# Two blocks of turned rows that leave on other queues, in a one-core encoder layer

## The chip, the cores and the metric

The kernel runs on one core of one Trainium2 chip. A core has TensorE (PE in the profile, with its weight loads as PEld), VectorE (DVE), ScalarE (ACT), GpSimd (POOL) and SyncE (SP), and 16 DMA engines that all queues share. The metric is device time in microseconds of one launch; the time before is the median of three runs.

## The reference

One layer of an encoder over 2048 tokens of width 1024, all in float32. After windowed and neighbourhood attention with gates, the part that matters here is the end of the layer:

```
x  = x + merged @ w_out
h2 = rms_norm(x, norm_mlp)
x  = x + square(relu(h2 @ w_up)) @ w_down      # w_up: 1024 x 4096
return rms_norm(x, norm_final)
```

## The kernel before

**Products.** A float32 product is made of three TensorE products of float32r halves: each operand is split into a high part (a cast on ACT, L280) and a low part (a subtraction on DVE, L281), and L284 to L286 multiply high by high, high by low and low by high. On top of that the large products are cut 2 x 2 and made of seven products in place of eight, from sums and differences of the blocks. For `h2 @ w_up` the seven are numbered 1 to 7 and taken in the order 1, 5, 6, 2, 7, 4, 3 (`up_quad`, L1309).

**The stretch around the change.** The 2048 tokens are four blocks of 512. In the last part of the stage of `w_out`, for the two last blocks (2 and 3), the finished rows x are stored to x2d (L173, on ACT's queue), their squares are summed (L223, ACT; L226, DVE), the power -1/2 is taken (L228, POOL), and the rows are scaled (L235, ACT). They are then turned, features to partitions, since w_up's products contract over features. `turned_out` (L239) turns one block in four steps g of 256 columns: four DVE transposes of 32 x 32 squares (L247) fill one tile of 128 x 1024, and four transfers of 128 KB (L255) write its four groups of 32 partitions to the block's matrix in DRAM, `h2d`, in pieces of 512 bytes. Blocks 0 and 1 went that way earlier, from one tile `ht` and with SP's queue. Blocks 2 and 3 go through `turned_last` (L1468), with POOL's queue:

- block 2 is turned into the memory of two gate tiles, `m2` and `m3` (L1461), beside the last product of w_out;
- block 3 is turned into four tiles `hu` (L1532, L1538), after that stage's memory (`s_m`) has been given back.

So each block takes 16 transfers of 128 KB. POOL is in order: what stands behind such a transfer on POOL (the powers of block 3, L228) waits until it is issued.

**Memory that passes on.** The products with w_up take over that memory. Their right operands are pages `ubh1` to `ubh7`, one pair (high, low) for each product of the first group of tokens (blocks 0 and 1). `up_homes` makes them at three places: `bh1`, `bh5` first; `bh6`, `bh2` and the page `rb` after `s_m` is given back (L1530), partly where m2 and m3 were; `bh7`, `bh4`, `bh3` after hu and the rows are given back (L1541). A page can be written only when the transfers that read the memory before have ended.

**Weights.** w_up is taken in eight groups q of 512 columns for each of the two groups m of tokens. `up_weights(q)` (L1153) loads group q as two tiles `uraw` of 1 MB on SP's queue, one group ahead (L1557); `up_left` makes the seven left operands `uwhla`, `uwhlb` of them, with sums `uS`. The ring `uraw` has five tiles, which also hold pages while the right operands are made.

**Order.** A scheduler sets each engine's order when the program is built, by its own estimates of the times; `tc.issue_after(x)` holds an instruction back until x is issued in that order. All waits are on semaphores that the framework places; the transfers of SP's and ACT's queues take turns on eight of them, and a transfer is not issued before the last one on its semaphore has landed. TensorE's order around here is: the end of w_out's products (tiles `pgl`), then group q = 0 of w_up with products 1, 5, 2, 6, 7, 4 and 3.

Of the kernel before, what the change touches and what calls it, by code (L numbers as in the profile page):

```python
# [22 lines left out]
P = 128  # L23
KC = D // P
NB = 4
BT = 512
# [66 lines left out]
def encoder_layer(ctx, tc, x, norm_mix, w_in, b_gate, sink, rpb, w_pa, w_pb, w_out,  # L93
                  norm_mlp, w_up, w_down, norm_final, dist_a, mask_b, out):
    nc = tc.nc
    V, A, G, PE, SY = nc.vector, nc.scalar, nc.gpsimd, nc.tensor, nc.sync
# [114 lines left out]
    last_dma = [None]  # L211
# [27 lines left out]
    def turned_out(d, ht, tiles, g, gain=None, queue=None):  # L239

        hv = ht.rearrange("p (j t c) -> p t j c", j=8, t=4)
        for t in range(4):
            V.transpose(out=hv[:, t], in_=tiles[t][:, g * 256 : (g + 1) * 256].rearrange("p (j c) -> p j c", j=8))  # L247
        h3 = ht.rearrange("p (j x) -> p j x", j=8)
        if gain is not None:
            (step, n), _ = gain.ap  # L250
            gv = bass.AP(gain.tensor, gain.offset + 8 * g, [[step, n], [1, 8], [0, P]])
            V.tensor_tensor(out=h3, in0=h3, in1=gv, op=ALU.mult)
        dv = d.rearrange("(j i) (a x) -> a i j x", i=32, a=4)
        for a in range(4):
            (queue or SY).dma_start(dv[a][:, 8 * g : 8 * g + 8], h3[32 * a : 32 * a + 32])  # L255

    def turned_gain(t, norm):

# [33 lines left out]
    def ring(stack, tag, shape, dt, bufs, side="right"):  # L292

        pl = pool(f"r_{tag}", side=side, stack=stack)
        return lambda: T(pl, shape, dt, tag, bufs)
# [62 lines left out]
    def in_weights(c, w):  # L358

        return [row_half(c, w, p) for p in range(2)]  # L360
# [285 lines left out]
    ws = in_weights(*QUADS[2])  # L646
# [53 lines left out]
    for q in range(2, len(QUADS)):  # L700
        prep = iter(())
        if q in (2, 3):
            prep = wo_parts(q - 2, own_v)
        elif q in (7, 8):
            prep = wo_parts(q - 5, own_x)
        next(prep, None)
        if q == 5:
            s_v.close()
            in_v2.pop()
            xp = {**pools(s_z, "right", ("xin",), "x2"), "st": cp}  # L710
        if q == 7:
            bias_tables()
        lf = list(in_left(ws, 256, (1, 2) if q == 2 else (), ORDER if q == 2 else ORDER_3))
        if q + 1 < len(QUADS):
            ws = in_weights(*QUADS[q + 1])
        if q in (5, 6):

            b = q - 3
            xt = x_tiles(xp, b, 3)
            normalised(xp, xt, Junk(), by_scalar=True)  # L720
        ops2.extend(lf if q == 2 else ())
        for n, _ in enumerate(quad2 if q == 2 else in_seeded(*QUADS[q], iter(lf), right)):
            for _ in range(2 if q == 8 else 1):
                next(prep, None)
            if q in (5, 6) and n < 4:
                turned_out(h1d[b - 2], in_e().rearrange("p k x -> p (k x)"), xt, n)
        for _ in prep:
            pass
# [381 lines left out]
    h2d = [dp.tile([D, BT], F32, name=f"h2d{b}") for b in range(NB)]  # L1110
# [39 lines left out]
        n_whl[0] += 1  # L1150
        return (up_rings["whla"] if n_whl[0] % 3 == 1 else up_rings["whlb"])()

    def up_weights(q):  # L1153
        ws = []
        for p in range(2):
            w = up_rings["raw"]()
            SY.dma_start(w, w_up[0][p * BT : (p + 1) * BT, q * BT : (q + 1) * BT].rearrange("(k p) f -> p k f", p=P))
            ws.append(w)
        return ws

    def up_left(ws, behind=None):

        out = {}
        for _ in up_left_steps(ws, out, behind):
            pass
        return out
# [40 lines left out]
    def parts_ahead(n):  # L1207

        src = h2d[2] if n == 1 else h2s_d[n]
        for k in range(4):  # L1210
            lo, hi = up_rings["chunk"](), up_rings["chunk"]()
            with tc.issue_after(stored[0]) if k == 0 and stored[0] else nullcontext():
                SY.dma_start(lo, src[k * P : (k + 1) * P, :])
            yield
            if n == 1:
                by_gain(lo, k)
            A.copy(hi.bitcast(F32R), lo)
            V.tensor_tensor(out=lo.bitcast(F32R), in0=lo, in1=hi, op=ALU.subtract)
            for z, t in enumerate((hi, lo)):
                SY.dma_start(h2p_d[n][z][k * P : (k + 1) * P, :], t)  # L1220

    def ahead(k):

        b = {}
        for j, p in ((0, 0), (1, 0), (1, 1), (0, 1)):
            b[p, j] = up_rings["chunk"]()
            with tc.issue_after(stored[0]):
                SY.dma_start(b[p, j], h2d[2 + j][p * BT + k * P : p * BT + (k + 1) * P, :])
            by_gain(b[p, j], 4 * p + k)
        t1, t3, t2, t4 = b[0, 0], b[0, 1], b[1, 1], b[1, 0]  # L1230
        for n, out, x, y in ((5, t1, t3, t1), (7, t3, t2, t3), (6, t2, t2, t1), (4, t4, t4, t2)):
            yield
            add(V, out, x, y, ALU.subtract)
            SY.dma_start(h2s_d[n][k * P : (k + 1) * P, :], out)
# [138 lines left out]
    def up_start():  # L1373

        up_homes("raw", "whla", "whlb", "bh1", "bh5", "S")
        rights, lf = up_right(0), {}
        next(rights)
        yield
        next(rights)
        ws = up_weights(0)  # L1380
        yield
        rest = up_left_steps(ws, lf)
        started.extend((rights, lf, rest))
        for _ in range(2):
            next(rest)
        yield
# [61 lines left out]
    def beside_out(m):  # L1448

        loads = load_y(1) if m == 0 else up_start()  # L1450
        for n in range(7):
            if m == 0 and n in (1, 3, 4, 6):
                state["y"] = next(loads)
            elif m == 1:
                if n < 2:
                    rows[1].extend(x_row(m, 1, 2 * n + t) for t in range(2))
                elif n < 5:
                    next(loads)
                elif n == 6:
                    free = [T(p4x, [P, 2, 2, BT], F32, f"m{t}", 1).rearrange("p a b c -> p a (b c)") for t in (2, 3)]  # L1460
                    turned_last(0, lambda g: free[g // 2][:, g % 2])  # L1461
            yield
# [5 lines left out]
    def turned_last(i, own):  # L1468

        for g in range(4):  # L1470
            turned_out(h2d[2 + i], own(g), rows[i], g, queue=G)

    state = {"y": next_y}
    rows = None
    for m in range(2):
# [5 lines left out]
        old, rows = rows, [[], []]  # L1481
# [23 lines left out]
        for f in range(8):  # L1505
            if m:
                i = f // 4
                turned_out(h2d[i], T(p4x, [P, 2 * BT], F32, "ht", 1), old[i], f % 4, gain)
            if 0 < f and f + early < 8:
                gated(f + early, 0)  # L1510
            gated(f, 1)
            add(V, ms[f // 2][:, f % 2], gates[f, 0], gates[f, 1])
            if f == 3:
                ready = [next(operands), next(operands)]
            if f >= 4 or m == 0:
                rows[1 - f // 4 if m else f // 4].append(x_row(m, 1 - f // 4 if m else f // 4, f % 4))
# [19 lines left out]
    for _ in rest:  # L1536
        pass
    turned_last(1, lambda t: hu())  # L1538
    s_hu.close()
    s_wo.close()  # L1540
    up_homes("bh7", "bh4", "bh3", "chunk")  # L1541
    for m in range(2):
        if m:
            right = next(rights)
            lf = up_left(up_weights(0))
        next(rights, None)
        ws = None
        for q in range(8):
            lf = up_left(ws, page_done[0] if m == 0 and q == 1 else None) if q else lf
            if m == 0 and q == 6:  # L1550
                rights = up_right(1)
                next(rights)
            spread = iter(())
            if m == 0 and 1 <= q < 7:
                spread = ahead(q - 2) if 2 <= q < 6 else parts_ahead(1 if q == 1 else 5)
            next(spread, None)
            if q < 7:  # L1557
                ws = up_weights(q + 1)
            up_quad(m, q, lf, right, spread)
    s_up.close()  # L1560

# [13 lines left out]
    rows = [ring(s_dn, tag, [P, BT], F32, 8) for tag in "XYZW"]  # L1575
# [107 lines left out]
    for n in (1, 6, 2, 7, 5, 3, 4):  # L1683
        for group in ((range(8),) if n != 4 else (range(4), range(4, 8))):
# [8 lines left out]
            last = []  # L1693
# [54 lines left out]
```

## Time and profile before

| | |
|---|---|
| median of three runs | 2658.98 us (2657.82 to 2659.52) |
| the profiled execution | 2660.67 us, span 2658.9 us |
| TensorE busy | 2573.6 us, 97% of the span |
| VectorE, ScalarE busy | 1624.8 and 1290.3 us |
| GpSimd busy | 394.0 us |
| HBM read and written | 349.51 and 174.13 MB |
| SP's, ACT's and POOL's transfers (q1, q10, q0) | 479.69, 28.32 and 15.73 MB |

Rows of a timeline give the start, the time, the engine, the line, the operation, output and input, how many, and in brackets the idle time before them and what ended it. `SPq` and `ACTq` rows are transfers as they are issued. A waits row says who waited for whom: total, how often, the longest. Names of tiles are given without their numbers, so `ubh` stands for the pages of all seven products.

### The profile page before, as it was taken

What the parts mean: (1) busy time and instruction counts of PE and PEld (TensorE: products, weight loads), DVE (VectorE), ACT (ScalarE), POOL (GpSimd) and SP (SyncE); (2) the same over time, 40 slices, a digit from 0 to 9 for tenths busy, and PEclk for the clock granted to TensorE, in tenths of its full rate; (3) what the DMA queues carried; (4) which work ended last, traced back from release to release, by engine and by line L of the source; (5) the groups of instructions that cost most, each with busy time, mean ns of one, the idle gap of its engine ahead of it and who ended that gap; (6) DMA issues with size and microseconds to landing.
All of it is one profiled execution on the core that took longest, in us unless ns stands there. A gap on an engine that the chain in (4) does not pass through costs nothing. (4 is left out here: it accounts for less than half of the span.)

```text
span 2658.9 us, 34486 instructions
## 1 busy us (share of the span) xinstructions
PE 2573.6 (97%) x12044; PEld 2132.8 (80%) x12044; DVE 1624.8 (61%) x2611; ACT 1290.3 (49%) x2319; POOL 394.0 (15%) x509
## 2 busy tenths in 40 slices
PE   7999999999999999999995999999999999999998
PEld 6878878777888887878884888888887888888887
DVE  7865566665544444476675676776566634555767
ACT  7356456666555555344344555554444332322444
POOL 0000233344555541000012000000000000000011
PEclk9999999999999999999997999999999999999999
DMA  5777694455876765778675655854436935445555
GB/s 182 253 241 209 223 297 135 113 151 148 236 219 186 192 161 162 242 246 272 197 264 177 221 200 202 290 200 155 143 118 258 323 116 179 143 147 170 186 188 170
DMA packets 342782, 525.94 MB, mean 198 GB/s; under 512 B 29624, under 2 KB 164920, under 8 KB 340432
## 3 DMA queue, kind: packets, MB, share of 16 engines
q1 hardware_dynamic: 324304, 479.69, 56.5%
q10 hardware_dynamic: 13248, 28.32, 2.9%
q0 software_dynamic: 5056, 15.73, 1.9%
q8 instruction: 95, 1.56, 0.2%
q14 instruction: 79, 0.65, 0.1%
HBM read 349.51 MB, written 174.13 MB: 197 GB/s over the span
## 5 line engine op out<-in xcount | busy, mean ns | idle before, releaser
L285 PE MATMUL b<-dwh,dah 128*128 128x512 f32 x896 | 348.7, 389 | 0.4 <-DVE dwh L281 0.4
L286 PE MATMUL b<-dwh,dah 128*128 128x512 f32 x896 | 347.8, 389 | 0.0
L284 PE MATMUL b<-dwh,dah 128*128 128x512 f32 x896 | 338.3, 389 | 1.6 <-ACT dwh L280 1.6
L280 ACT CAST dah<-da 128x1024 fp32r<-128x1024 f32 (+1 forms) x128 | 120.9, 945 | 368.3 <-PE b L286 246.1
L281 DVE TENSOR_TENSOR dah<-da,dah 128x1024 fp32r<-128x1024 f32 (+1 forms) x128 | 139.1, 1089 | 219.0 <-ACT dah L280 216.9
L284 PE MATMUL b<-ubh,uwhlb 128*128 128x512 f32 x592 | 231.3, 391 | 29.0 <-ACT ubh L280 27.4
L285 PE MATMUL b<-ubh,uwhlb 128*128 128x512 f32 x592 | 231.3, 391 | 1.3 <-DVE ubh L281 1.3
L286 PE MATMUL b<-ubh,uwhlb 128*128 128x512 f32 x592 | 229.8, 390 | 0.0
L200 PE MATMUL mm<-hT,whl 128*128 128x512 f32 x544 | 219.0, 403 | 2.6 <-ACT hT L754 2.6
L201 PE MATMUL mm<-hT,whl 128*128 128x512 f32 x544 | 215.0, 395 | 0.6 <-DVE hT L755 0.6
L202 PE MATMUL mm<-hT,whl 128*128 128x512 f32 x544 | 215.4, 396 | 0.0
L284 PEld LDWEIGHTS b<-dwh,dah 128*128 128x128 f32 x896 | 168.1, 188 | 37.0 <-ACT dwh L280 2.1
L285 PEld LDWEIGHTS b<-dwh,dah 128*128 128x128 f32 x896 | 168.2, 188 | 35.7 <-DVE dwh L281 0.8
L286 PEld LDWEIGHTS b<-dwh,dah 128*128 128x128 f32 x896 | 168.2, 188 | 34.9
L284 PE MATMUL zb<-zh,zwhl 128*128 128x512 f32 x476 | 186.2, 392 | 5.4 <-DVE zc L277 2.2
L285 PE MATMUL zb<-zh,zwhl 128*128 128x512 f32 x476 | 186.1, 391 | 0.0
L286 PE MATMUL zb<-zh,zwhl 128*128 128x512 f32 x476 | 185.0, 390 | 1.1 <-DVE zwhl L281 1.1
L277 DVE TENSOR_TENSOR uc<-b,uc 128x512 f32<-128x512 f32 x160 | 109.1, 688 | 123.4 <-PE b L286 117.4
L284 PEld LDWEIGHTS b<-ubh,uwhlb 128*128 128x128 f32 x592 | 111.4, 189 | 53.4 <-ACT ubh L280 28.2
L285 PEld LDWEIGHTS b<-ubh,uwhlb 128*128 128x128 f32 x592 | 111.5, 188 | 25.7 <-DVE ubh L281 2.5
L286 PEld LDWEIGHTS b<-ubh,uwhlb 128*128 128x128 f32 x592 | 111.6, 188 | 23.0
L286 PE MATMUL b<-ubh,uwhla 128*128 128x512 f32 x304 | 118.1, 389 | 1.9 <-DVE uwhla L281 1.9
(270 smaller groups left out, 5830.2 us busy)
## 6 DMA issues: line engine op xcount, KB each, us to landing
at<-uc SPq DMA_DIRECT2D x224, 256.0 KB
da<-at SPq DMA_DIRECT2D x96, 512.0 KB
dw<-in_w_down_dram SPq DMA_DIRECT2D x160, 256.0 KB
uraw<-in_w_up_dram SPq DMA_DIRECT2D x32, 1024.0 KB
pgl<-wo_d SPq DMA_DIRECT2D x28, 1024.0 KB
raw<-in_w_in_dram SPq DMA_DIRECT2D x34, 512.0 KB
zraw<-in_w_in_dram SPq DMA_DIRECT2D x16, 1024.0 KB
z<-zg SPq DMA_DIRECT2D x64, 256.0 KB
```

The lines of the kernel that those rows point to most:

```text
L200: PE.matmul(ps, lh, rh, start=first, stop=False)
L201: PE.matmul(ps, lh, rl, start=False, stop=False)
L202: PE.matmul(ps, ll, rh, start=False, stop=last)
L277: return eng.tensor_tensor(out=out, in0=a, in1=b, op=op).ins
L280: A.copy(hi, src)
L281: return eng.tensor_tensor(out=lo, in0=src, in1=hi.bitcast(F32), op=ALU.subtract).ins
L284: PE.matmul(ps, lh, rh, start=first, stop=False, skip_group_check=True)
L285: PE.matmul(ps, lh, rl, start=False, stop=False, skip_group_check=True)
L286: PE.matmul(ps, ll, rh, start=False, stop=last, skip_group_check=True)
```

## The change

The transfers of blocks 2 and 3 are issued on SP's and on ACT's queue in turn (groups 0 and 2 of 32 partitions on SP, 1 and 3 on ACT) and no longer on POOL's. `turned_out` keeps the last of them that SP issues, and the load of the weights of the second group (`up_weights(1)` for the first group of tokens) is held back in the order until that one, which is block 3's, is issued. Nothing of what is computed changes. Line numbers after the changed places move by three or four.

```diff
@@ turned_out
         for a in range(4):
-            (queue or SY).dma_start(dv[a][:, 8 * g : 8 * g + 8], h3[32 * a : 32 * a + 32])
+            q = queue[a % 2] if queue else SY
+            last = q.dma_start(dv[a][:, 8 * g : 8 * g + 8], h3[32 * a : 32 * a + 32]).ins
+            if q is SY:
+                last_dma[0] = last
@@ up_weights
-    def up_weights(q):
+    def up_weights(q, behind=None):
         ws = []
         for p in range(2):
             w = up_rings["raw"]()
-            SY.dma_start(w, w_up[0][p * BT : (p + 1) * BT, q * BT : (q + 1) * BT].rearrange("(k p) f -> p k f", p=P))
+            with tc.issue_after(behind) if behind else nullcontext():
+                SY.dma_start(w, w_up[0][p * BT : (p + 1) * BT, q * BT : (q + 1) * BT].rearrange("(k p) f -> p k f", p=P))
             ws.append(w)
         return ws
@@ turned_last
         for g in range(4):
-            turned_out(h2d[2 + i], own(g), rows[i], g, queue=G)
+            turned_out(h2d[2 + i], own(g), rows[i], g, queue=(SY, A))
@@ the loop over groups
             if q < 7:
-                ws = up_weights(q + 1)
+                ws = up_weights(q + 1, last_dma[0] if m == 0 and q == 0 else None)
             up_quad(m, q, lf, right, spread)
```

In the built program the instructions around these places are ordered anew, from the end of w_out's products to the third group of w_up: SP has eight transfers of m ahead of the load of `urb` and eight of hu ahead of the second group's weights; ACT has eight of m ahead of the four stores to x2d, and eight of hu between the evictions of product 2 and the casts of ubh3 and ubh7; POOL has the four powers alone; and TensorE takes product 6 ahead of product 2. Every other part of each engine's order is as before.

## The prediction

> **What bounds the kernel now.** I read the page's second part first, for where TensorE (PE) is not busy.
>
> ```profile
> PE 2573.6 (97%) x12044; PEld 2132.8 (80%) x12044; DVE 1624.8 (61%) x2611; ACT 1290.3 (49%) x2319; POOL 394.0 (15%) x509
> ...
> PE   7999999999999999999995999999999999999998
> ...
> PEclk9999999999999999999997999999999999999999
> ```
>
> PE is the bound nearly everywhere; the one deep hole, in busy time and in granted clock, is the 22nd slice, 1396 to 1462 us. There the rows of blocks 2 and 3 leave, and the first of the 16 groups of products with w_up begins. The windows view gives the hole its size (columns: stretch, length, then each engine's busy time, the granted clock, DMA share, GB/s):
>
> ```profile
> 1393.00:1420.00 27.00, 23.00 (x98) 17.72 (x96) 18.05 (x30) 15.29 (x21) 10.49 (x17) 1.00 0.65 193
> 1420.00:1446.50 26.50, 0.02 (x2) 0.02 (x1) 7.92 (x9) 4.59 (x8) 7.56 (x13) 0.57 0.69 192
> 1446.50:1470.00 23.50, 23.46 (x94) 18.68 (x95) 15.49 (x19) 13.85 (x21) 0.00 (x0) 0.91 0.47 167
> ```
>
> 26.5 us without a product, 1.0% of the span. The waits view of 1380 to 1480 us says which waits, and the timeline how they chain:
>
> ```profile
> PE b L284 <- ACT ubh L280: 27.4, 2, 26.5
> POOL h2d L255 <- issue: 27.7, 15, 6.8
> ACT ubh L280 <- DMA h2d<-hu: 21.9, 1, 21.9
> DVE ubh L281 <- DMA h2d<-m: 6.1, 1, 6.1
> ACT xr L235 <- POOL st L228: 5.7, 2, 4.5
> ```
> ```profile
> 1404.04 0.39 PE L284 MATMUL b<-ubh,uwhla 128*128 128x512 f32 x1
> ...
> 1384.90 1.84 POOL L255 DMA_DIRECT2D h2d<-m  x3 [3.98 <-DVE m L247]
> ...
> 1407.19 3.42 POOL L228 TENSOR_TENSOR st<-st,power 128x1 f32<-128x1 f32 x4
> 1417.86 1.78 POOL L255 DMA_DIRECT2D h2d<-hu  x3 [7.24 <-DVE hu L247]
> ...
> 1442.79 0.58 POOL L255 DMA_DIRECT2D h2d<-hu  x1 [0.62 <-issue]
> ...
> 1408.50 2.27 ACT L235 ACTIVATE xr<-xr,st 128x1024 f32<-128x1024 f32 x2 [4.48 <-POOL st L228]
> ...
> 1445.39 1.99 ACT L280 CAST ubh<-uraw 128x1024 fp32r<-128x1024 f32 x2 [21.91 <-DMA h2d<-hu]
> ...
> 1446.48 1.22 PE L284 MATMUL b<-ubh,uwhlb 128*128 128x512 f32 x2 [26.48 <-ACT ubh L280]
> ```
>
> Backwards: PE resumes at 1446.48 because ACT casts ubh (the page of product 7) at 1445.39; the cast waits until hu, whose memory that page takes over, has left for h2d; and its 16 transfers, ready from 1417.86, are issued one by one by POOL until 1443.4. POOL's idle is "issue": it waits for nothing in the profile but its own queue. The block takes 27.5 us, 1417.86 to 1445.39.
>
> How much of that is transfer? DMA view, 1417 to 1446 us (queue: packets, MB, share of 16 engines):
>
> ```profile
> q1 hardware_dynamic: 2076, 4.06, 43.3%
> ...
> q0 software_dynamic: 768, 2.10, 29.7%
> ```
>
> hu's 2.10 MB (q0) used 29.7% of 29 us = 8.6 us of all engines; weights of w_up (q1, mostly) 12.6 us; 7.8 us nothing.
>
> **The change part by part.**
>
> *m's 16 transfers (block 2) move from POOL to SP and ACT, eight each.* The trace has this shape on SP's queue already: four such transfers of h2d<-ht, after which DVE may overwrite ht.
>
> ```profile
> 1219.68 1.86 SPq L255 DMA_DIRECT2D h2d<-ht  x4
> ...
> 1227.00 14.41 SPq L255 DMA_DIRECT2D h2d<-ht  x8
> ...
> 1223.69 1.10 DVE L247 STREAM_TRANSPOSE ht<-xr 128x256 f32<-128x256 f32 x3 [1.63 <-DMA h2d<-ht]
> ...
> 1236.88 1.42 DVE L247 STREAM_TRANSPOSE ht<-xr 128x256 f32<-128x256 f32 x4 [1.60 <-DMA h2d<-ht]
> ...
> q1 hardware_dynamic: 1088, 0.52, 56.4%
> ```
>
> The last row is 1219.6 to 1224 us with that traffic alone: 56.4% of 4.4 us = 2.48 us of all engines per four. From issue to release took 4.0 us, so 1.5 us is start and landing; issuing costs 0.46 us each. Sixteen: 1.5 + 4 x 2.48 = 11.4 us alone. The other end is the second case: beside other transfers four took 9.9 us (1227.0 to 1236.9). I take the first: at 1384.9 nothing else moves until x2d's stores, now behind m on ACT's queue, and the load of urb, behind m on SP's. So m has left by 1384.9 + 11.4 = 1396.3; now POOL turns from issuing it to the powers only at 1407.2.
>
> What is queued behind: ACT issues its eight in order, each with a wait for an earlier transfer on the same of eight semaphores, so it is held until about half of the block is gone, 1391 to 1394, and its squares start there and not at 1388. POOL is free, so the four powers (1407.19 now) come as soon as the squares are there. In the built order of the changed kernel ACT then casts ubh6 at m's release, and product 6 goes ahead of product 2. PE reaches that place at 1404.0 as now (its first row above); ubh6 (cast 2.0 us, DVE's low half after it) is ready by 1400. The small stalls (3 us of the 4.0 idle in the first window) go, but that time would only be waited at the next place.
>
> *When do hu's transposes end?* From 1396.3 the built order gives ACT 20 instructions and DVE 32, durations from these rows:
>
> ```profile
> 1388.41 0.63 ACT L223 ACTIVATE junk<-xr 128x512 bf16<-128x512 f32 x1
> ...
> 1389.16 0.63 ACT L223 ACTIVATE junk<-xr 128x512 bf16<-128x512 f32 x1
> ...
> 1402.49 1.05 ACT L280 CAST uwhla<-uraw 128x1024 fp32r<-128x1024 f32 x1
> 1403.44 0.58 ACT L1336 COPY uc<-b 128x512 f32<-128x512 f32 x1
> ...
> 1413.51 2.19 ACT L235 ACTIVATE xr<-xr,st 128x1024 f32<-128x1024 f32 x2
> ...
> 1418.52 2.00 ACT L280 CAST ubh<-uraw 128x1024 fp32r<-128x1024 f32 x2 [1.88 <-DVE hu L247]
> ```
> ```profile
> L247 DVE STREAM_TRANSPOSE hu<-xr 128x256 f32<-128x256 f32 x16 | 5.4, 406 | 0.5 <-ACT xr L235 0.5
> ...
> L277 DVE TENSOR_TENSOR urb<-urb,uraw 128x1024 f32<-128x1024 f32 x2 | 2.4, 1216 | 0.0
> L281 DVE TENSOR_TENSOR uwhla<-uraw,uwhla 128x1024 fp32r<-128x1024 f32 x2 | 2.4, 1198 | 0.0
> L281 DVE TENSOR_TENSOR ubh<-urb,ubh 128x1024 fp32r<-128x1024 f32 x2 | 2.4, 1222 | 6.1 <-DMA h2d<-m 6.1
> ...
> L226 DVE SCALAR_TENSOR_TENSOR st<-st 128x1 f32<-128x1 f32 x1 | 0.2, 158 | 1.9 <-ACT junk L223 1.9
> ```
>
> ACT: four half casts of pages 4.0, three of weights 3.2, seven half squares at 0.75 5.3, two copies 1.2, four scalings 4.4: 18.1 us. DVE: 16 transposes 5.4, ten subtractions over 1024 columns 12.1, two over 512 columns 1.4 (0.69 each, row below), four small 0.6: 19.5 us. With no wait between them DVE ends at 1415.8. Walking both lists, each instruction at the later of its engine's and its input's time, I get 1418.8 for the last transpose and 1417.8 for the first quarter, the same as now (1417.86). So the first half of the change gives nothing by itself; a later release of m would move all of this one for one.
>
> *hu's 16 transfers (block 3) move likewise.* Issue from 1417.8 on SP; ACT stands at its eight about 1.2 us later, after two evictions and a cast. Nothing is behind POOL any more. 1417.8 + 11.4 = 1429.2, and I add 1 us for ACT's late start: released at 1430.2. Bounds: hu's 8.6 us alone would give 1427.9; full mixing with the weights, below, 1439.
>
> *The second group's weights go behind them.* Their issue on SP now follows hu's eight and waits for the ninth transfer of the block to land (one semaphore serves both), 1417.8 + 1.5 + 9 x 0.62 = 1424.9. Two loads of 1 MB behind seven of hu's transfers still to go (4.3 us), then 12.6 us / 4.06 MB x 2.1 MB = 6.5 us: landed by 1435.7. What needs them first is DVE's sum uS, after the four low halves of ubh7 and ubh4:
>
> ```profile
> 1448.74 2.35 DVE L281 TENSOR_TENSOR ubh<-urb,ubh 128x1024 fp32r<-128x1024 f32 x2
> 1453.39 2.74 DVE L277 TENSOR_TENSOR uc<-b,uc 128x512 f32<-128x512 f32 x4 [2.29 <-PE b L286]
> ...
> 1454.52 1.05 ACT L280 CAST uwhlb<-uraw 128x1024 fp32r<-128x1024 f32 x1 [5.25 <-PE b L286]
> ```
>
> Those end 1448.74 + 2.35 - 1445.39 = 5.7 us after the cast begins, so at 1435.9: just covered. But the three sums of 1.2 us, which now run inside PE's hole, then stand ahead of the eviction uc that product 4 waits for: done 5.7 + 3.5 + 0.7 = 9.9 us after the cast, while PE ends product 7 at 1454.5 - 1445.39 = 9.1. **A new wait of 0.8 us**; each us that the weights are later than 1435.9 adds one.
>
> *Sum.* Cast at 1430.2, PE 1.1 us later as now: 1431.3 instead of 1446.48, 15.2 us earlier; less 0.8: **14.4 us**. PE still idles some 16 us: from 1404.0 on products 6 and 2 have 48 matmuls, which the first window's row prices at 23.00 / 98 = 0.235 us, so they end at 1415.3. So the slow restart is paid as now. Behind it PE is the bound in every slice, so the gain reaches the end. The profiled execution took 2660.67 us, 1.69 over the median of the runs, 2658.98: 2646.3, or **2644.6** as a median.
>
> *What speaks against it.* By the row above, engines and bytes stay the same, and only the idle 7.8 us and the order against the weights can be won. [...]
>
> **The rivals.**
>
> *A, the weights mix in.* If the weights' pieces take turns with what is left of hu, hu ends when both are through: 1417.8 + 8.6 + 12.6 = 1439.0, a gain of 6.4 less 0.8, 2653.4. For it: q0 and q1 were busy together now. Against: SP issues the weights only after its own eight. [...]
>
> *B, slower: ACT is held at m.* If m's block goes like the case with other loads, 4 x 9.9 = 39.6 us, m leaves at 1424.5, the walk above ends 28.2 us later, at 1447.0, and PE resumes at 1459.5: 13 us slower, 2672. It decides from a block of m of 26.6 us on. For it: x2d's 2.1 MB and urb's load are there, and ACT has no other work to go to. Against: both are queued behind m.
>
> *C, no change.* The page's memory waits for something else as late, or uS's weights land 14 us late, at 1450. The cast's row names only hu; weights issued by 1425 would need 25 us. 2659.
>
> *D, more.* POOL's powers come 10 us earlier; if DVE's transposes followed at once, hu would start near 1412: 2639. Against: DVE's order has the ten subtractions among them.
>
> **How the numbers follow.** Forecast (gain 9 to 18) 0.68, A (gain 4 to 9) 0.13, B 0.09, C 0.04, D 0.06. The predicted time is the forecast's. Its own range is 2641 to 2650; with A the range is 2640 to 2654, leaving out B, C and most of D. A measurement can tell about 0.2%, 5.3 us, from no change: faster 0.68 + 0.06 + most of A = 0.86, slower B = 0.09, the same 0.05.
>
> **What would show it.** POOL's issues gone from the waits; h2d<-m released near 1396; the powers before 1416; hu issued from about 1418, the cast of ubh7 near 1430 and PE's idle near 16 us; then a small wait of PE for DVE's uc. Wrong if hu's block takes over 20 us, if the transposes end after 1425, or if DVE waits for uraw.

## The result, and the profile after

The changed kernel takes 2649.41 us in the median of six runs (2644.34 to 2652.0), beside 2659.26 us for the kernel before (six runs, with the three of the table above, 2657.82 to 2666.73): a ratio of 0.9956, interval 0.9941 to 0.9971, so it is faster by 0.44%. A second set is the first experiment below (0.9942). The profiled execution took 2652.0 us, its span 2650.2. Its page, the same three rows as shown of before (busy time; busy tenths in 40 slices; granted clock):

```profile
PE 2578.1 (97%) x12044; PEld 2138.1 (81%) x12044; DVE 1625.9 (61%) x2611; ACT 1293.3 (49%) x2319; POOL 376.5 (14%) x477
...
PE   7999999999999999999997999999999999999998
...
PEclk9999999999999999999998999999999999999999
```

The 22nd slice is busy to 7 tenths where it was 5, and its clock went from 7 to 8. It is still the one dip in TensorE's row between the first slice and the last. The waits of 1380 to 1480 us say what is left of the hole and what is new (who waits, for whom: total, times, longest):

```profile
PE b L287 <- ACT ubh L283: 15.3, 1, 15.3
...
ACT junk L223 <- DMA x2d<-xr: 15.6, 1, 15.6
...
PE b L287 <- DVE uc L280: 3.3, 1, 3.3
...
DVE uS L280 <- DMA uraw<-in_w_up_dram: 1.8, 1, 1.8
```

POOL's 27.7 us of "issue" are gone and PE's 26.5 us have become 15.3. In their place stand ScalarE, 15.6 us without work, a wait of PE for DVE's uc, and a wait of DVE for the weights. The timeline shows how they follow on each other (line numbers three or four higher than before):

```profile
1386.31 7.95 ACTq L256 DMA_DIRECT2D h2d<-m  x8
1394.35 5.72 ACTq L173 DMA_DIRECT2D x2d<-xr  x4
1400.11 0.63 ACT L223 ACTIVATE junk<-xr 128x512 bf16<-128x512 f32 x1 [15.57 <-DMA x2d<-xr]
...
1418.58 2.72 DVE L247 STREAM_TRANSPOSE hu<-xr 128x256 f32<-128x256 f32 x8
...
1420.35 7.49 SPq L256 DMA_DIRECT2D h2d<-hu  x8
...
1427.93 1.92 SPq L1161 DMA_DIRECT2D uraw<-in_w_up_dram  x2
...
1431.11 2.00 ACT L283 CAST ubh<-uraw 128x1024 fp32r<-128x1024 f32 x2 [0.63 <-DMA h2d<-hu]
...
1432.21 1.22 PE L287 MATMUL b<-ubh,uwhlb 128*128 128x512 f32 x2 [15.31 <-ACT ubh L283]
...
1438.65 1.22 DVE L280 TENSOR_TENSOR uS<-uraw,uraw 128x1024 f32<-128x1024 f32 x1 [1.83 <-DMA uraw<-in_w_up_dram]
...
1443.14 0.76 PE L287 MATMUL b<-ubh,uwhlb 128*128 128x512 f32 x1 [3.35 <-DVE uc L280]
```

Read from the top: ScalarE stands at its eight transfers of m for 7.95 us and at four stores to x2d for 5.72 us more, and sums its first square only at 1400.11 (1387.65 before). hu is issued at 1420.35 (1417.86 before, but this execution was already 1.8 us late at 1387, ahead of anything that was changed). Then hu's block takes 10.8 us, from 1420.35 to the cast at 1431.11, where it took 27.5. PE restarts at 1432.21, 14.3 us earlier than before, 16.1 against the 1.8. At the end only 8.6 of the 14.3 are left. The windows view shows where they went (stretch, length, busy time of PE, PEld, DVE, ACT, POOL, granted clock, DMA share, GB/s):

```profile
1393.00:1421.30 28.30, 23.90 (x106) 19.47 (x104) 19.15 (x35) 19.06 (x32) 4.00 (x4) 1.00 0.45 143
1421.30:1432.20 10.90, 0.00 (x0) 0.00 (x0) 3.48 (x5) 4.25 (x7) 0.00 (x0) 0.53 1.00 231
1432.20:1440.00 7.80, 7.54 (x24) 5.34 (x24) 5.93 (x6) 2.97 (x4) 0.00 (x0) 0.78 1.04 374
1440.00:1443.10 3.10, 0.00 (x0) 0.00 (x0) 3.07 (x4) 0.88 (x1) 0.00 (x0) 0.90 1.05 403
1443.10:1450.00 6.90, 6.86 (x18) 5.40 (x19) 3.51 (x5) 2.91 (x5) 0.00 (x0) 0.55 1.03 382
```

Two slow stretches of PE in place of one: after the long hole at a clock of 0.78 (7.8 us, 1.7 lost), and, after a pause of only 3.35 us, at 0.55 (6.9 us, 3.1 lost). These clocks are means over the stretch; in windows of 0.85 us the granted clock is 0.50 or 1.00, with values between only where it changes. Pause and second slow stretch together are 6.5 us, a little more than what was given back.

### The profile page after: what moved, and what is told of

Its sections match the earlier page's. It is cut to its first block, busy times and chain, and to the rows that moved or that the text cites. A ratio compares the mean times of both kernels' runs of the same rounds, so it can differ in the third digit from the quotient of the medians.

```text
span 2650.2 us, 34483 instructions
## 1 busy us (share of the span) xinstructions
PE 2578.1 (97%) x12044; PEld 2138.1 (81%) x12044; DVE 1625.9 (61%) x2611; ACT 1293.3 (49%) x2319; POOL 376.5 (14%) x477
## 4 chain that ended last, share of the span: by engine, by line
PE 79%; DMA 7%; DVE 5%; ACT 2%; issue 2%; SPq 1%; POOL 0%; ACTq 0%; POOLq 0%; DVEq 0%
PE b L288 15%; PE b L289 15%; PE b L287 15%; PE mm L201 4%; PE mm L200 4%; PE mm L202 4%; PE b L200 2%; PE av L1033 2%; PE b L201 2%; PE b L202 2%; PE zb L289 2%; PE zb L287 2%; PE zb L288 2%; PE s L994 2%; PE pt L1022 2%
## 5 line engine op out<-in xcount | busy, mean ns | idle before, releaser
L287 PE MATMUL b<-ubh,uwhlb 128*128 128x512 f32 x592 | 232.4, 393 | 20.3 <-ACT ubh L283 15.3
L287 PEld LDWEIGHTS b<-ubh,uwhlb 128*128 128x128 f32 x592 | 112.2, 190 | 44.8 <-ACT ubh L283 15.7
L289 PEld LDWEIGHTS b<-ubh,uwhlb 128*128 128x128 f32 x592 | 112.2, 189 | 23.5
L200 PEld LDWEIGHTS mm<-hT,whl 128*128 128x128 f32 x544 | 103.0, 189 | 21.7 <-ACT hT L757 4.1
```

Of the source, the lines that this page charges most:

```text
L200: PE.matmul(ps, lh, rh, start=first, stop=False)
L287: PE.matmul(ps, lh, rh, start=first, stop=False, skip_group_check=True)
L289: PE.matmul(ps, ll, rh, start=False, stop=last, skip_group_check=True)
```

## The experiments

After the result three things were open. Is the new wait for uc, with the slow stretch behind it, worth the 5 us that the trace gives it? Does holding back the weights do anything? And does the second queue help, or does ScalarE's stand cost more than it brings? Each block of rows was therefore changed by itself.

All profiles drift by up to 4 us before the changed place (offsets against the kernel before at 1387 us: from -4.3 to +2.8), so the steps are compared inside one profile. Here m is the first transfer of block 2, "square" ScalarE's first square of block 3's rows, hu the first transfer of block 3, "cast" the cast of ubh7; the idle time is PE's before product 7. "Gain in trace" is how much sooner than in the profile before TensorE's last product starts, counted from the execution's own offset at 1387 us. Times in us, the median and the ratio with its interval from the timed runs; the kernel before had 2661.0 in the set of the next four rows behind the changed kernel's first, 2660.62 in the set of the four after them, and 2661.23 beside the last.

| kernel | m to square | m to hu | hu to cast | m to cast | PE idle | gain in trace | median | ratio |
|---|---|---|---|---|---|---|---|---|
| before | 2.8 | 33.0 | 27.5 | 60.5 | 26.5 | - | 2659.26 | 1 |
| changed | 13.8 | 34.1 | 10.8 | 44.8 | 15.3 | 10.5 | 2649.41 | 0.9956 [0.9941, 0.9971] |
| changed, again | 12.8 | 33.4 | 10.6 | 44.0 | 14.5 | 12.3 | 2647.58 | 0.9942 [0.9928, 0.9955] |
| weights not held | 12.5 | 32.8 | 11.4 | 44.1 | 14.6 | 12.6 | 2645.99 | 0.9939 [0.9926, 0.9951] |
| sums late | 10.9 | 32.3 | 10.7 | 42.9 | 13.4 | 17.3 | 2647.30 | 0.9941 [0.9928, 0.9953] |
| SyncE alone | 3.2 | 24.2 | 11.6 | 35.8 | 4.1 | 24.0 | 2637.44 | 0.9906 [0.9893, 0.9920] |
| m SyncE, hu both | 3.2 | 24.2 | 10.6 | 34.8 | 3.2 | 24.2 | 2637.82 | 0.9915 [0.9902, 0.9928] |
| m both, hu SyncE | 12.2 | 32.4 | 10.9 | 43.3 | 13.7 | 16.5 | 2647.25 | 0.9945 [0.9933, 0.9957] |
| m GpSimd, hu both | 2.8 | 33.7 | 10.7 | 44.5 | 8.9 | 14.3 | 2646.37 | 0.9944 [0.9932, 0.9955] |
| m both, hu GpSimd | 13.2 | 33.9 | 23.8 | 57.7 | 28.2 | 3.0 | 2657.90 | 0.9991 [0.9983, 1.0000] |
| x2d by SyncE | 8.1 | 31.4 | 10.7 | 42.1 | 12.6 | 16.9 | 2646.21 | 0.9936 [0.9922, 0.9950] |

The medians follow the column "m to cast": before to "m SyncE, hu both" it falls by 25.7 us and the time by 22.8 (2660.62 in that set to 2637.82).

The gain in the trace leaves the drift out. From 1500 us on every profile keeps its distance to the profile before within 0.4 us, so what an execution gained between 1387 and 1500 us is what reaches its end. It is one execution of each kernel, though, and the two of the changed kernel differ by 1.8 us.

### The changed kernel again

No edit.

> The changed kernel once more, beside the experiments. Both theories: 2649 us, PE idle 15.3 us before product 7 and 3.4 us before product 4, as in its first profile.

2647.58 us beside 2661.0 (0.9942, 0.9928 to 0.9955). The same picture, with the wait for uc once more:

```profile
1441.39 0.77 PE L287 MATMUL b<-ubh,uwhlb 128*128 128x512 f32 x1 [3.42 <-DVE uc L280]
```

So the two new waits belong to the kernel and are no accident of one execution.

### The weights not held back

```diff
-                ws = up_weights(q + 1, last_dma[0] if m == 0 and q == 0 else None)
+                ws = up_weights(q + 1)
```

> The queues as changed, the second group's weights not held back: in the built order SP issues their two loads before hu's eight. Theory (the queues bought the gain, the hold gave part of it back): the weights load between 1406 and 1420 us, when the changed kernel's DMA engines stand idle, so DVE's sum uS does not wait, PE's wait for uc before product 4 shrinks from 3.4 us to under 1 and its clock is not halved a second time (2.5 us); hu's block grows by at most 3 us; 2 to 6 us faster than the changed kernel, about 2645. Rival (the hold bought the gain, since weights and hu shared the engines before): hu's block grows from 11 us towards 20, and the time goes to 2655 or more.

The second group's weights go ahead of hu's transfers on SyncE's queue (SyncE's row), and PE's wait for uc before product 4 is gone, but another one comes later, when the next products want uc (PE's row):

```profile
1409.76 1.58 SPq L1161 DMA_DIRECT2D uraw<-in_w_up_dram  x2
...
1475.84 0.47 PE L287 MATMUL b<-ubh,uwhla 128*128 128x512 f32 x1 [2.47 <-DVE uc L280]
```

This pause of 2.47 us has a slow stretch behind it too, 3.4 us at a clock of 0.50. hu's block takes 11.4 us against 10.6 to 10.8 with the weights behind it, and the time is 2645.99 us, 1.6 less than the changed kernel's in this set, with intervals that overlap almost wholly. Holding the weights back is worth nothing that these runs can tell. SyncE alone without the hold, and POOL's queue with the weights held behind it, were not run.

### The sums of the weights behind product 7's eviction

DVE's sums of the new weights (uS), which stood ahead of the eviction uc that product 4 waits for, are held behind it:

```diff
-    page_done = [None]
+    page_done, evicted = [None], [None]
...
-                    last = plus(c22[a], z[a], c22[a])
+                    last = evicted[0] = plus(c22[a], z[a], c22[a])
...
-            lf = up_left(ws, page_done[0] if m == 0 and q == 1 else None) if q else lf
+            lf = up_left(ws, evicted[0] if m == 0 and q == 1 else None) if q else lf
```

> The changed kernel, with DVE's sums for the second group put behind the eviction of product 7 in the order; nothing else. Theory: PE's 3.4 us before product 4 and the half clock after it (2.5 us) go, about 6 us: 2643. Rival (the shortfall lies before the restart, and what is taken away here is only waited at the next place): another wait of the same size at the start of group 1, within 1.5 us of the changed kernel.

The wait of 3.4 us and the second slow stretch are gone (windows view, columns as above: one stretch at 0.65, then full clock):

```profile
1428.90:1436.00 7.10, 7.00 (x20) 5.14 (x21) 4.63 (x4) 2.85 (x4) 0.00 (x0) 0.65 1.02 343
1436.00:1446.00 10.00, 10.00 (x46) 8.20 (x45) 8.96 (x11) 5.90 (x9) 0.00 (x0) 1.00 1.05 395
```

In the profiled execution nearly all of the gain reaches the end (17.5 us at the restart, 16.8 at the last product, where the changed kernel's second profile kept 11.9 of 16.5). The wait that the rival named, at the start of the next group, is 0.77 us. From the restart to the last product this execution lost 0.7 us of its gain and the changed kernel's two profiles 5.6 and 4.6, so in the traces the pause and its slow stretch cost 4 to 5 us. But the median, 2647.30, is 0.3 us from the changed kernel's. The profiled execution (2643.87) is one of the two quickest of five, which reach up to 2648.5. So the trace shows the mechanism and a price, and the medians do not show it; their intervals reach about 3.5 us to either side, which can hide it. What the other executions of this kernel did was not seen, since one execution of each is profiled. This stays open.

### All 32 transfers on SyncE

```diff
-            turned_out(h2d[2 + i], own(g), rows[i], g, queue=(SY, A))
+            turned_out(h2d[2 + i], own(g), rows[i], g, queue=(SY, SY))
```

> All 32 transfers of m and hu on SP's queue, none on ACT's. Theory (the 16 DMA engines are the limit, a second queue saves issue time only): hu's block takes 11 to 13 us as with two queues; ACT is not held from 1386 to 1400, squares and scalings come earlier, hu starts some 6 us earlier and the time is 2640 to 2646. Rival (the second queue is worth its place): hu's block takes 15 us or more and the time is not under the changed kernel's 2649.

2637.44 us (0.9906, 0.9893 to 0.992), 10.1 us below the changed kernel in the same set and more than was expected:

```profile
1387.28 14.80 SPq L256 DMA_DIRECT2D h2d<-m  x16
...
1390.49 0.63 ACT L223 ACTIVATE junk<-xr 128x512 bf16<-128x512 f32 x1 [5.58 <-DVE xr L280]
...
1411.03 1.41 DVE L247 STREAM_TRANSPOSE hu<-xr 128x256 f32<-128x256 f32 x4
...
1411.49 9.14 SPq L256 DMA_DIRECT2D h2d<-hu  x16
...
1423.04 2.00 ACT L283 CAST ubh<-uraw 128x1024 fp32r<-128x1024 f32 x2 [6.62 <-DMA h2d<-hu]
...
1424.14 1.22 PE L287 MATMUL b<-ubh,uwhlb 128*128 128x512 f32 x2 [4.12 <-ACT ubh L283]
```

ScalarE takes its first square 3.2 us after m's first transfer, waiting only for the product's rows (DVE xr), and the four powers on POOL follow the squares, the last at 1402.4. hu's transposes end at 1412.4 and its transfers start 24.2 us after m's, where the changed kernel needs 34. That is not because m leaves faster: beside the stores to x2d, the cast that waits for m starts 17.9 us after m's first transfer, and 12.3 us after it in the profile with the sums late. PE's hole shrinks to 4.1 us. The block of hu takes 11.6 us from one queue, 10.6 to 10.8 from two, and the DMA view of 1411.4 to 1423.1 (queue: packets, MB, share of 16 engines) shows why the second queue has little to win: the engines are busy 87% of it.

```profile
q1 hardware_dynamic: 4416, 2.23, 87.4%
```

### Which block's half on ScalarE costs

m on SyncE alone, hu by halves:

```diff
-            turned_out(h2d[2 + i], own(g), rows[i], g, queue=(SY, A))
+            turned_out(h2d[2 + i], own(g), rows[i], g, queue=(SY, A) if i else (SY, SY))
```

> The block of m leaves all 16 transfers on SyncE; hu's still goes by halves on SyncE and ScalarE. Theory (what the second queue costs, 2647.6 us against 2637.4 us with SyncE alone, is ScalarE standing still behind its transfers of m, not behind those of hu): ScalarE squares from about 1390 on as with SyncE alone, hu's transposes end near 1412, TensorE's idle stretch before product 7 is 4 to 6 us, and the time is 2635 to 2640. Rival (ScalarE's half of hu is what costs): the idle stretch stays above 10 us and the time is 2645 to 2650.

2637.82 us (0.9915, 0.9902 to 0.9928), as the theory says and as SyncE alone. The timeline, and below it the DMA view of 1409.6 to 1420.3, hu's block (SyncE's and ScalarE's queue):

```profile
1385.46 13.96 SPq L256 DMA_DIRECT2D h2d<-m  x16
...
1388.67 0.63 ACT L223 ACTIVATE junk<-xr 128x512 bf16<-128x512 f32 x1 [5.59 <-DVE xr L280]
...
1409.65 7.53 SPq L256 DMA_DIRECT2D h2d<-hu  x8
...
1421.37 1.22 PE L287 MATMUL b<-ubh,uwhlb 128*128 128x512 f32 x2 [3.20 <-ACT ubh L283]
```
```profile
q1 hardware_dynamic: 2250, 1.20, 45.8%
q10 hardware_dynamic: 2176, 1.05, 43.6%
```

With both queues the 16 engines are busy 89% of the block. ScalarE's half of hu harms nothing and saves 0.9 us of the block against SyncE alone; in the time that cannot be told from nothing.

The mirror, m by halves and hu on SyncE alone:

```diff
-            turned_out(h2d[2 + i], own(g), rows[i], g, queue=(SY, A))
+            turned_out(h2d[2 + i], own(g), rows[i], g, queue=(SY, SY) if i else (SY, A))
```

> The mirror of the run before: m by halves on SyncE and ScalarE, hu with all 16 transfers on SyncE. Theory (ScalarE held at m costs the 10 us): as the changed kernel, ScalarE held until about 1398 to 1400, the idle stretch before product 7 13 to 16 us, 2645 to 2650. Rival (ScalarE's half of hu costs): 2635 to 2640.

2647.25 us (0.9945, 0.9933 to 0.9957), as the changed kernel:

```profile
1390.94 3.93 ACTq L173 DMA_DIRECT2D x2d<-xr  x4
1394.91 0.63 ACT L223 ACTIVATE junk<-xr 128x512 bf16<-128x512 f32 x1 [14.53 <-DMA x2d<-xr]
...
1427.10 1.22 PE L287 MATMUL b<-ubh,uwhlb 128*128 128x512 f32 x2 [13.74 <-ACT ubh L283]
```

The two runs settle which half it is: the 10 us hang on m's half on ScalarE and not on hu's (7.5 to 12 us by the gains in the traces). With m's half gone the scheduler also orders ScalarE and DVE anew: ScalarE takes all eight squares ahead of the cast of ubh6, where the changed kernel puts casts and copies between them. How much of the 10 us is the standing and how much the order was not parted.

### Which block carries the gain over the kernel before

hu alone by halves, m on GpSimd as before:

```diff
-            turned_out(h2d[2 + i], own(g), rows[i], g, queue=(SY, A))
+            turned_out(h2d[2 + i], own(g), rows[i], g, queue=(SY, A) if i else (G, G))
```

> Only hu's block leaves by halves on SyncE and ScalarE; m's stays on GpSimd as before. Theory (the changed kernel's gain is the shorter block of hu alone, m's faster block being undone by ScalarE's hold, so that hu's transposes end near 1418.5 with either): restart after hu about 1431, 2646 to 2651, as the changed kernel. Rival (m's half carries part of the gain): 2652 to 2657, with hu's transposes later than 1421.

2646.37 us (0.9944, 0.9932 to 0.9955): the whole gain of the changed kernel. ScalarE is free here from the start, and yet hu comes no earlier, since now the powers stand behind m's transfers on POOL, as they did before. PE reaches the hole 36.7 us after m's first transfer here and 30.6 in the changed kernel (two pauses of 1.74 and 1.55 us, and 6.8 us at a mean clock of 0.52, come before it), so its idle time is shorter, but the restart is no sooner:

```profile
1388.42 0.63 ACT L223 ACTIVATE junk<-xr 128x512 bf16<-128x512 f32 x1 [5.55 <-DVE xr L280]
...
1409.02 3.59 POOL L228 TENSOR_TENSOR st<-st,power 128x1 f32<-128x1 f32 x4
...
1419.39 7.61 SPq L256 DMA_DIRECT2D h2d<-hu  x8
...
1431.23 1.22 PE L287 MATMUL b<-ubh,uwhlb 128*128 128x512 f32 x2 [8.85 <-ACT ubh L283]
```

m alone by halves, hu on GpSimd as before:

```diff
-            turned_out(h2d[2 + i], own(g), rows[i], g, queue=(SY, A))
+            turned_out(h2d[2 + i], own(g), rows[i], g, queue=(G, G) if i else (SY, A))
```

> Only m's block leaves by halves on SyncE and ScalarE; hu's stays on GpSimd as before. Theory (m's half is worth nothing with ScalarE held): hu's transposes still end near 1418 to 1421, its block takes the 27 us of before, restart near 1446 to 1449, 2657 to 2662, as before. Rival (m's half carries part of the gain): 2649 to 2655.

2657.9 us in twelve runs (0.9991, 0.9983 to 1.0): as before. hu's block took 23.8 us and not the 27 expected. Below the timeline stands the DMA view of that block, 1414.1 to 1437.9 (SyncE's and GpSimd's queue):

```profile
1380.21 7.65 SPq L256 DMA_DIRECT2D h2d<-m  x8
...
1393.43 0.63 ACT L223 ACTIVATE junk<-xr 128x512 bf16<-128x512 f32 x1 [14.68 <-DMA x2d<-xr]
...
1414.09 1.85 POOL L256 DMA_DIRECT2D h2d<-hu  x3 [2.99 <-DVE hu L247]
...
1437.86 1.99 ACT L283 CAST ubh<-uraw 128x1024 fp32r<-128x1024 f32 x2 [20.23 <-DMA h2d<-hu]
```
```profile
q1 hardware_dynamic: 1768, 3.46, 42.9%
q0 software_dynamic: 768, 2.10, 36.8%
```

So the gain of the change is hu's block off POOL. What makes the block long there was not taken apart. POOL issues with gaps of up to 5.6 us, and 3.46 MB of other transfers, mostly weights, pass in the meantime (3.69 MB in the kernel before); in the run with the weights not held 1.35 MB passed beside hu's two halves, and the block still took 11.4 us. Moving m's block from POOL to SyncE and ScalarE is worth nothing as it was done: the squares now stand where the powers stood.

### The stores to x2d on SyncE

As the changed kernel, but the four stores that ScalarE issued right behind m go to SyncE:

```diff
-                        flush(1)
+                        flush(1, SY if (m, n) == (1, 4) else A)
             if n in (4, 3):
-                flush()
+                flush(0, SY if (m, n) == (1, 4) else A)
```

> As the changed kernel, with m and hu by halves on SyncE and ScalarE, but the four writes of x2d that ScalarE issued right behind its eight transfers of m are issued by SyncE. Theory (ScalarE's hold is the sum of its issues: some 7.5 to 8 us for eight transfers of m and 3 to 6 us for four writes of x2d behind them): ScalarE's first square comes about 8 us after m's first issue in place of 10 to 14, hu's transposes end 3 to 6 us sooner, TensorE's idle stretch before product 7 is 8 to 11 us in place of 13 to 16, and the time is 2641 to 2645. Rival (ScalarE waits for the data path to come free, whoever issues: the scaling of xr in place may not start until the write of x2d has read xr, and that write now queues behind SyncE's own eight): no gain, 2646 to 2650, with ScalarE or DVE waiting for x2d<-xr instead.

```profile
1386.92 8.01 ACTq L256 DMA_DIRECT2D h2d<-m  x8
1394.98 0.63 ACT L223 ACTIVATE junk<-xr 128x512 bf16<-128x512 f32 x1 [9.99 <-DMA h2d<-m]
...
1418.30 7.56 SPq L256 DMA_DIRECT2D h2d<-hu  x8
...
1430.07 1.22 PE L287 MATMUL b<-ubh,uwhlb 128*128 128x512 f32 x2 [12.55 <-ACT ubh L283]
```

The hold is the sum of what ScalarE issues, as the theory had it: the first square comes 8.1 us after m's first transfer, right behind the eighth. But 5.7 us less of hold (8.1 for 13.8) brought hu only 2.7 us nearer (31.4 for 34.1, where no hold gives 24.2), the hole stayed at 12.6 us where 8 to 11 were expected, and 2646.21 us (0.9936, 0.9922 to 0.995) lies above the expected 2641 to 2645 and cannot be told from the changed kernel. So with 8 us of hold left, 7.2 of the 9.9 us are still lost. That casts and copies then stand between the late squares in ScalarE's order may be why; it was not tried. Neither case of the expectation holds whole: the hold is as the theory says, the time as the rival says, for another reason than the rival's (no wait of ScalarE or DVE for block 3's x2d<-xr is in this trace). This trace gained 16.9 us, 4.6 to 6.4 more than the changed kernel's two: 2.0 to 2.8 of them at the restart, the rest behind it, where its pause for uc is 1.52 us and the clock stays at 1.00.

## Why the prediction came out as it did

The time, 2649.41 and 2647.58 us in two sets, lies in the range 2640 to 2654, 3 to 5 us above the 2644.6 predicted. Of the 14.4 us predicted, the two profiles gained 10.5 and 12.3, each from its own offset. Step by step:

- **hu's block, 27.5 to 12.4 us: right, and it is the gain.** It took 10.8 us. The term of 11.4 from four transfers in 2.48 us was good; the 1 us added for ScalarE's late start was not needed. That hu alone on these queues gives the whole gain (2646.37) confirms the step by itself.
- **"The first half of the change gives nothing by itself": right** (m alone: 0.9991). The reason given was wrong in part. The prediction let ScalarE's hold cost nothing, because it took the walk of both engines' lists to start only when m is released, at 1396.3. The squares do not need m's release. With ScalarE free they start 3 us after m's first transfer, the scheduler puts hu's transposes ahead of part of the subtractions, and hu starts 10 us sooner. This is rival D's mechanism (2639, given 0.06), which the prediction excluded by the order of DVE in this build; with m on SyncE alone the order is another and it happens.
- **ScalarE "held 1391 to 1394": mis-sized.** It was held until 1400.1 (1398.3 without the drift). The missed term is the four stores to x2d right behind the eight transfers, 5.7 us in that trace, 3.2 to 5.4 in the five others with this hold. Even so hu came only 0.7 us later than the predicted 1418.8 plus drift for the last transpose (1421.3), since the walk behind the hold took 21.2 us where 22.5 were worked out.
- **Restart 15.2 us earlier: 16.1** against the drift.
- **Weights "just covered", landed 1435.7 for a need at 1435.9: missed by 1.8 us.** Counted from hu's first transfer the weights were there after 18.3 us (predicted 17.9), but the need came after 16.5 us (predicted 18.1), because hu's block was 1.6 us shorter than predicted. The need stood 5.7 us behind the cast, as worked out. A wait of DVE for uraw was one of the prediction's own signs of being wrong; it came, at this size.
- **"A new wait of 0.8 us": the step that failed.** It was 3.35 us, 1.83 of the difference from those weights, and the prediction left out that such a pause slows PE once more: 6.9 us at a clock of 0.55. Both together are 6.5 us in the trace, and beside the trace of the run with the sums late they cost 4 to 5 us; in the medians they cannot be seen.
- **The slow restart "paid as now": right once**, 1.7 us lost at 0.78 beside 2.1 (23.5 us at 0.91) before.
- **The rivals.** A, the weights mixing in, did not come: hu's block took 10.8 us with the weights behind it and 11.4 with them ahead. B, ScalarE held at m for 40 us, did not come either, but its mechanism is there at a third of that size and cost 10 us of a possible gain: its price was set against the kernel before, where nothing of it shows, and not against the same change without ScalarE. C did not come. D came with ScalarE out of the way.

What a second queue is worth here, the traces show: one queue takes 10.9 to 11.6 us and two take 10.6 to 10.8 us for the same 2.1 MB with the weights behind them, and the engines are busy 87% (SyncE alone) and 89% (m on SyncE, hu by halves) of the block. The gain comes from leaving POOL's queue, not from having two others. The time of the issuing engine is a cost of its own, here 10 us of ScalarE's place in the chain.

The version that beats both kernels is the one with all 32 transfers on SyncE, 2637.44 us, or equally the one with m on SyncE and hu by halves.

## What to carry to other kernels

Before a transfer is moved to an engine that computes, read what stands behind it on that engine and who waits for that: here eight transfers and four stores kept ScalarE 11 to 14 us from the squares that the next block needs, and with SyncE, which had only one load waiting behind them, issuing all of m's block the kernel was 10 us shorter. Compare a change with its nearest variants too, not only with the kernel before, since a standstill that moves from one engine (GpSimd's powers) to another (ScalarE's squares) shows as no loss. And a load that is "just covered" has no cover: when the step ahead of it gets faster, its need comes earlier by as much (here 1.6 us).

## What the chip showed that was not expected

- A short pause of PE can cost a slow stretch behind it, and the length of the one does not follow the other. Behind pauses of 2.47 us (weights not held), 3.20 us (m SyncE, hu both), 3.35 and 3.42 us (the changed kernel twice) the granted clock was 0.50 for 3.4, 6.8, 6.8 and 3.4 us. Behind single pauses of 1.28 us (m both, hu SyncE), 1.52 us (x2d by SyncE) and 1.62 us (m GpSimd, hu both) it stayed at 1.00. The windows behind the pauses of 2.47 and 1.28 us (columns as above):

```profile
1476.50:1479.90 3.40, 3.40 (x10) 2.62 (x9) 2.99 (x4) 3.31 (x5) 0.00 (x0) 0.50 0.96 260
...
1436.50:1443.00 6.50, 6.43 (x28) 5.37 (x29) 4.58 (x6) 3.54 (x6) 0.00 (x0) 1.00 1.05 387
```

So 2.47 us was enough here, and a single 1.62 us was not. What decides it in between, and whether the slow stretch lasts 3.4 or 6.8 us, these runs do not show.

- The issue of a 128 KB transfer with pieces of 512 bytes held ScalarE 1.0 us each (7.95 us for eight) and a store to x2d, which takes 0.33 us there when nothing is ahead of it, 1.4 us each behind them (5.72 us for four).
- The same 2.1 MB take 10.6 to 11.6 us from SyncE's and ScalarE's queues and 23.8 to 27.5 us from GpSimd's, there with 3.5 to 3.7 MB of other transfers beside them.
- Profiled executions stand up to 7 us apart before the changed code is reached (offsets of -4.3 to +2.8 us at 1387 us, against the kernel before), with the same instructions up to there. The timed runs spread as much (8.9 us over six runs of the kernel before, 7.7 us over six of the changed kernel), so 2 or 3 us are beyond these medians. From 1500 us on the distances between the profiles stay as they are, within 0.4 us.
